# A hybrid RWKV, attention and expert block: gating shared by two engines, and four changes of order

## The chip, the cores and the metric

The kernel runs on one core of a Trainium2 chip. The metric is the device time of one execution in microseconds (us). Before the change it was 2046.03 us, the median of three runs (2045.47 to 2049.38). The engines are TensorE (PE; PEld is its weight load), VectorE (DVE), ScalarE (ACT), GpSimd (POOL) and SyncE (SP), which issues most DMA transfers.

## The reference

The input is 256 tokens of width 2048. One layer is computed: a combined input projection, causal attention with 8 heads of 128, an RWKV-7 time mix with 16 heads of 64, an output projection, and then PEER, a retrieval over 16384 experts of one neuron each, which fills most of the time:

```python
q = (xt @ wq).reshape(T, H, 2, PEER_HALF)
s = jnp.einsum('thpc,hpnc->thpn', q, sub_keys)
sv, si = lax.top_k(s, K)                      # K = 16, of 128 keys, twice
cand = (sv[:, :, 0, :, None] + sv[:, :, 1, None, :]).reshape(T, H, K * K)
best, bi = lax.top_k(cand, K)
expert = (i1 * PEER_NKEYS + i2)
gates = jax.nn.softmax(best, axis=-1)
hpre = jnp.einsum('cd,chkd->chk', xc, u[ec])
act = jax.nn.gelu(hpre, approximate=False) * gc
y = jnp.einsum('chk,chkd->cd', act, v[ec])
```

So for each token 8 heads choose 16 experts each; an expert's gelu is multiplied by its gate, and its row of `v` is added with that weight. A final norm ends it.

## The kernel before, in words

Products in float32 are made of three products of split operands: ScalarE copies a weight into the high part `whi` (L204), VectorE subtracts to get the low part `wlo` (L205), and TensorE multiplies. `prefetch()` does this for a half of 512 KB at a time; three pairs of split buffers stand ready in the stage of the experts, and the list `halves` fixes the order in which weights come from memory through SyncE.

**Stage 1, 0 to about 540 us.** The input projection. `products()` computes three column blocks for each RWKV pair of heads `j` and three for each attention head `h`; each finished one starts a generator (`rwkv`, `attn`) that is put into the list `live`. After every few matmuls of the projection `step_all()` advances up to four generators by a step. First come all eight RWKV blocks, then the eight attention heads. SyncE also writes zeros into `rows_d`, a table in memory (`clear`).

**Stage 2, 540 to 735 us.** Output projection, queries, scores and the first choices.

**Stage 3, 736 to about 1568 us.** `hidden()` multiplies all 16384 expert rows of `u`, 128 keys `i2` of 128 experts each. A key takes 32 pairs of a 512-column (L240) and a 256-column matmul (L242), in two halves of weights. Then ScalarE and VectorE add the two banks into `part` (L1137, L1138), and in the next key ScalarE's gelu (L1122) writes it into the buffer `A` of eight keys. Those buffers, the rows `at` to be scattered and the gates `gt` share one pool of 16 slots.

Beside it three generators run by credit. With each yield of `hidden()` every one gains STEP times its rate, and pays by the number that it yields:

- `both_choices` finds each token's experts (VectorE for the most part).
- `tables` builds for each half of the tokens (a tile `t`) a table of gates over all 128 x 128 experts: VectorE compares (`marks`, L937 and L939), ScalarE weights, TensorE multiplies, GpSimd sums (L951 to L959). Then `places` sorts the experts that are in use: those of the first tile alone, of the second alone, and of both.
- `scatter` handles a key at a time, once its gelu is done. `gated` multiplies the gelus by the gates (L1093), and an indirect DMA issued by GpSimd (L1107) writes the rows to their places in `rows_d`. For every seventh key a new tile `at` is taken and GpSimd copies the seven expert numbers into it (L1085); the seven rows stand side by side in the tile, 256 values and a number each. For every eighth key it loads gates (`gt`, L1075). The last two keys are gated by VectorE and stay in SBUF.

The framework's scheduler sets the final order of each engine's queue from the program and the dependencies, and puts the waits in. An engine runs its queue in order.

**Stage 4, to the end.** Sums over the experts, in 2 blocks from SBUF and 108 blocks of 128 experts (28 for the first tile, 28 for the second, 52 for both). A block's rows are read by SyncE (L1200), its `v` rows are gathered by an indirect DMA of GpSimd (L1205), split (L248, L249) and multiplied (L1192 to L1194) into eight banks. The order ends with blocks for the second tile alone. Then comes a run-time loop over further blocks (L1264), whose count is read from memory and which runs no trip here. The end (L1277 to L1297) adds the banks to the residual, takes the norm and writes the output.

Of the kernel before, what the change touches and what calls it, by code (L numbers as in the profile page):

```python
# [13 lines left out]
I32 = mybir.dt.int32  # L14
# [7 lines left out]
P = 128  # L22
# [132 lines left out]
def block_kernel(ctx: ExitStack, tc: tile.TileContext, x, cols, consts, w_lora, w_gate, w_rkv, w_qkv,  # L155
# [22 lines left out]
    halves = []  # L178
    for i in range(2):
        halves += [(w_lora[m, i].rearrange("p k c -> p (k c)"), HK * LOR) for m in range(2)]  # L180
    for w, n in ((w_gate, 2), (w_rkv, 3 * RJ), (w_qkv, 3 * AH)):
        halves += [(w[m, i].rearrange("p k c -> p (k c)"), HK * P) for m in range(n) for i in range(2)]
    KP = (4, 5, 6, 7, 0, 1, 2, 3)
    halves += [(w_out[m, i].rearrange("p k c -> p (k c)"), 1024) for m in range(4) for i in KP]
    if stage >= 3:
# [447 lines left out]
    def clear(n):  # L633
        for _ in range(n):
            i = len(zero)
            if i < BT // P // 8:
                zero.append(nc.sync.dma_start(gv[:, 8 * i:8 * i + 8, :], zt.unsqueeze(1).to_broadcast([P, 8, ROW])))

    def products():
        pss = [bank(b, [P, S]) for b in ("pw", "px")]  # L640
        for n, _ in enumerate(together([ps[:LOR] for ps in pss], LOR, xhk, xlk)):
            if n == 4:
                nc.sync.dma_start(kb, consts[:, 0:384])
            yield
        nc.sync.dma_start(kr, consts[:, 384:])
        nc.vector.tensor_scalar(bo64, bones, 1.0 / 64, None, op0=ALU.mult)
        psg = [bank("ch", [P, S]) for _ in range(2)]
        yield from gemm(psg[0], P, xhk, xlk)
        for n, _ in enumerate(gemm(psg[1], P, xhk, xlk)):
            if n == 1:  # L650
                first_norm()
                for i in range(2):
                    mixed(pss[i], LOR, cc(C_MW, i), lor[:LOR, i, :])
                mixed(psg[0], P, cc(C_MG, 0), lor[:, 2, :])
            yield
        mixed(psg[1], P, cc(C_MG, 1), lor[:, 3, :])
        state["pools"] = [spl, spl, spare[0]]
        for j in range(RJ):
            while len(live) > 4:
                step_all()  # L660
            got = []
            for i, mu in enumerate((C_MR, C_MK, C_MV)):
                ps = bank("gm")
                yield from gemm(ps, P, xhk, xlk)
                dst = tmp("rkv"[i], "rkv"[i])[:, :S]
                mixed(ps, P, cc(mu, j), dst)
                if j == 0 and i == 0:
                    nc.scalar.activation(lor[:, 2:4, :], lor[:, 2:4, :], AF.Sigmoid)
                    nc.scalar.activation(lor[:LOR, 0, :], lor[:LOR, 0, :], AF.Tanh)
                got.append(dst)  # L670
            live.append(rwkv(j, *got))
            clear(2)
        state["pools"] = [spl]
        for h in range(AH):
            while len(live) > 4:
                step_all()
            got = []
            for i in range(3):
                ps = bank("gm")
                yield from gemm(ps, P, xhk, xlk)  # L680
                dst = tmp("qkv"[i] + "a", "rkv"[i])[:, :S]
                nc.vector.tensor_tensor(dst, ps, rstd1, op=ALU.mult)
                got.append(dst)
            live.append(attn(h, got))
            clear(1)

    def step_all(most=4):
        for g in list(live[:most]):
            if next(g, 0) == 0:
                live.remove(g)  # L690
# [232 lines left out]
    def table(t):  # L923


        while t not in chosen:
            yield 0
        tr = chosen[t]
        b3 = [P, NB, P]
# [75 lines left out]
    def places():  # L1005
# [39 lines left out]
        for t, n, base in ((0, C0, 0), (1, C1, B1)):  # L1045
            V.scalar_tensor_tensor(rank[t], sums[t], off[:, t:t + 1], alone[t], op0=ALU.add, op1=ALU.subtract)
            V.scalar_tensor_tensor(inside[t], rank[t], float(n * P), alone[t], op0=ALU.is_lt, op1=ALU.mult)
            V.tensor_tensor(mid, mid, inside[t], op=ALU.subtract)
            V.scalar_tensor_tensor(tmp_, rank[t], float(base), inside[t], op0=ALU.add, op1=ALU.mult)
            V.tensor_tensor(pos, pos, tmp_, op=ALU.add)  # L1050
            yield 1.5
        V.tensor_tensor_scan(sums[2], ones, mid, 0.0, op0=ALU.mult, op1=ALU.add)
        V.tensor_copy(tot[:, 2:3], sums[2][:, P - 1:P])
        ps = ranks((2, 1))
# [25 lines left out]
    def gated(i2, eng=nc.gpsimd):  # L1080

        if i2 % 7 == 0:
            rows[0] = big("at")
            n = min(7, NKEY - i2)
            eng.tensor_copy(rows[0][:, 0:n * ROW].rearrange("p (n c) -> p n c", c=ROW)[:, :, T].bitcast(I32),  # L1085
                                  eint[:, i2:i2 + n])
        g = gates_of(i2 // 8)
        if i2 % 8 == 1:
            gates_of(i2 // 8 + 1)
            gts.pop(i2 // 8 - 1, None)  # L1090
        at = rows[0][:, i2 % 7 * ROW:(i2 % 7 + 1) * ROW]
        k = i2 % 8
        eng.tensor_tensor(at[:, 0:T].rearrange("p (q t) -> p q t", q=KT),  # L1093
                          As[i2 // 8][:, k, :].rearrange("p (q t) -> p q t", q=KT),
                          g.rearrange("p q (t b) -> p q t b", b=8)[:, :, :, k], op=ALU.mult)
        return at

    def scatter():
        while "places" not in chosen:
            yield 0  # L1100
        gates_of(0)
        yield 0
        for i2 in range(NKEY - DN):
            while hid["n"] <= i2:
                yield 0
            at = gated(i2)
            s_ = nc.gpsimd.indirect_dma_start(  # L1107
                out=rows_d, out_offset=bass.IndirectOffsetOnAxis(ap=place[:, i2:i2 + 1], axis=0),
                in_=at, in_offset=None)
            for z_ in done:  # L1110
                tc.declare_no_dep(s_.ins, z_.ins, reason="other rows")
            for z_ in zero:
                tc.add_manual_dep(s_.ins, z_.ins.name, SYNC, reason="zeros first")
            done.append(s_)
            yield 1.5


    summed = []
# [24 lines left out]
    def both_choices():  # L1143
        yield from finding
        for t in (1, 0):
            yield from choose(t)

    def tables():
        for t in (1, 0):
            yield from table(t)  # L1150
        yield from places()

    STEP = 1.44
    beside = [[both_choices(), 0.55, 0.0], [tables(), 0.38, 0.0], [scatter(), 1.0, 0.0]]

    def run(b, most=None):
        while b[2] > 0 and (most is None or most > 0):
# [85 lines left out]
    for k in range(len(order) + 5):  # L1243
# [13 lines left out]
        if k >= 5:  # L1257
            j = k - 5
            for t in order[j][1]:
                block((t,), *cut[j], ends[t] == j)  # L1260

    count = nc.values_load(nblk[0:1, 0:1], min_val=0, max_val=128,
                           skip_runtime_bounds_check_because="a count of at most 16384 experts in blocks of 128")
    with tc.For_i(MID, count, 1) as i:  # L1264
        ag, _ = rows_at(i * P + BM)
        block((0, 1), *divided(ag, gather(ag)), True)

    gf = mp.tile([P, D], F32, tag="ml", name="gf")
    nc.gpsimd.dma_start(gf, final_g.rearrange("(o d) -> o d", o=1).to_broadcast([P, D]))
# [53 lines left out]
```

## Time and profile before

| what | value |
|---|---|
| median of three runs | 2046.03 us |
| profiled execution | 2048.21 us |
| its span in the profile | 2046.3 us |
| TensorE busy | 1935.7 us (95%) |
| VectorE busy | 1437.7 us (70%) |
| ScalarE busy | 1062.9 us (52%) |
| GpSimd busy | 712.1 us (35%) |
| DMA | 443.91 MB, 217 GB/s over the span |

The span is what the profile's rows cover; the execution's own time is 1.9 us longer, for what lies around it. Busy shares are means over stages that differ, so they only say where to look: TensorE first. A stage is then read by itself, by the busy time of each engine in it, by what TensorE waited for, and by the instructions around a wait. `out<-in` names the tiles that an instruction writes and reads; idle time stands with the engine and line that ended it.

### The profile page before, as it was taken

To read this page: it belongs to the slowest core of one execution; us is meant where nothing else is said; L and a number is where in the kernel's file an instruction comes from. 1 tells how busy PE (TensorE), PEld (TensorE's weight loads), DVE (VectorE), ACT (ScalarE), POOL (GpSimd) and SP (SyncE) were. 2 spreads that over 40 slices of the span, in tenths; PEclk is the share of its full clock that TensorE was granted. 3 is DMA by queue.
4 is the path that set the end of the run, shared out by engine and by line. 5 is a ranking of instruction groups with operands and counts; after the bars stand their busy time and mean duration, and the time that the engine had idled before them with its cause. 6 is when DMAs were issued, how large, how long until landed. Compare 5 with 4: busy or idle time off the path is not lost. (4 is left out here: it accounts for less than half of the span.)

```text
span 2046.3 us, 31447 instructions
## 1 busy us (share of the span) xinstructions
PE 1935.7 (95%) x11804; PEld 1723.3 (84%) x11804; DVE 1437.7 (70%) x2090; ACT 1062.9 (52%) x1696; POOL 712.1 (35%) x654
## 2 busy tenths in 40 slices
PE   7888999999999999999999999887998999999996
PEld 6788999999879998878888888776887788888885
DVE  6766878766556888999878866544755666666665
ACT  4534554345455444677676744433444555555554
POOL 7211211100000000023424269998986333333322
PEclk9999999999999999999999999998999999999998
DMA  8999322225576666556666678786888887878783
GB/s 248 258 247 246 98 87 87 88 83 146 190 227 198 184 180 188 173 175 197 215 195 217 196 237 264 248 267 229 270 267 271 343 284 280 296 286 293 281 297 141
DMA packets 135291, 443.91 MB, mean 217 GB/s; under 512 B 14369, under 2 KB 52257, under 8 KB 118497
## 3 DMA queue, kind: packets, MB, share of 16 engines
q1 hardware_dynamic: 106992, 289.24, 47.7%
q0 software_dynamic: 28144, 152.65, 20.4%
q8 instruction: 93, 1.52, 0.3%
q14 instruction: 62, 0.50, 0.1%
HBM read 380.07 MB, written 61.76 MB: 216 GB/s over the span
## 5 line engine op out<-in xcount | busy, mean ns | idle before, releaser
L205 DVE TENSOR_TENSOR wlo<-raw,whi 128x1024 fp32r<-128x1024 f32 (+1 forms) x408 | 569.6, 1402 | 301.1 <-ACT whi L204 291.9
L240 PE MATMUL ps_gm<-nx,whi 128*128 128x512 f32 x2048 | 731.8, 400 | 24.9 <-ACT whi L204 21.9
L204 ACT ACTIVATE whi<-raw 128x1024 fp32r<-128x1024 f32 (+1 forms) x408 | 429.5, 1055 | 384.2 <-issue 89.5
L242 PE MATMUL ps_gm<-nx,wlo 128*128 128x256 f32 x2048 | 579.4, 283 | 14.2 <-DVE wlo L205 14.2
L240 PEld LDWEIGHTS ps_gm<-nx,whi 128*128 128x128 f32 x2048 | 387.8, 189 | 112.6 <-ACT whi L204 22.6
L242 PEld LDWEIGHTS ps_gm<-nx,wlo 128*128 128x128 f32 x2048 | 390.3, 191 | 20.1 <-DVE wlo L205 19.7
L249 DVE TENSOR_TENSOR vlo<-vraw,vhi 128x2048 fp32r<-128x2048 f32 x108 | 247.9, 2297 | 151.6 <-ACT vhi L248 146.1
L248 ACT ACTIVATE vhi<-vraw 128x2048 fp32r<-128x2048 f32 x108 | 205.9, 1913 | 156.3 <-DVE vlo L249 146.8
L1205 POOL DMA_INDIRECT vraw<-in_v_dram,ag x108 | 145.1, 1343 | 294.8 <-PE ps_gm L1194 210.0
L218 PE MATMUL ps_gm<-xh,whi 128*128 128x256 f32 x640 | 192.7, 301 | 0.8 <-ACT whi L204 0.8
L220 PE MATMUL ps_gm<-xh,wlo 128*128 128x256 f32 x640 | 185.1, 289 | 3.2 <-DVE wlo L205 3.1
L219 PE MATMUL ps_gm<-xl,whi 128*128 128x256 f32 x640 | 185.6, 290 | 0.0
L1107 POOL DMA_INDIRECT rows_d<-at,place x126 | 169.5, 1345 | 36.9 <-POOL at L1093 15.8
L951 POOL TENSOR_TENSOR mt<-gc 128x1024 f32<-128x1024 f32 x16 | 39.7, 2482 | 345.5 <-ACT gc L979 345.5
L1122 ACT ACTIVATE A<-part 128x256 f32<-128x256 f32 x128 | 53.1, 415 | 166.7 <-DVE part L1138 131.3
L1093 POOL TENSOR_TENSOR at<-A,gt 128x256 f32<-128x256 f32 x126 | 129.2, 1041 | 5.4 <-DMA gt<-gate_d 3.6
L220 PEld LDWEIGHTS ps_gm<-xh,wlo 128*128 128x128 f32 x640 | 122.8, 192 | 4.6 <-DVE wlo L205 4.2
L218 PEld LDWEIGHTS ps_gm<-xh,whi 128*128 128x128 f32 x640 | 122.9, 192 | 1.9 <-ACT whi L204 1.2
L219 PEld LDWEIGHTS ps_gm<-xl,whi 128*128 128x128 f32 x640 | 122.9, 192 | 0.7
L807 POOL DMA_DIRECT2D skb<-in_sk_dram x16 | 8.6, 540 | 250.7 <-ACT mh L248 167.7
L945 ACT ACTIVATE ob<-ob,pick 128x128 f32<-128x128 f32 x256 | 83.9, 390 | 19.6 <-DVE ob L937 19.6
L373 POOL TENSOR_TENSOR df<-ext 128x256 f32<-128x256 f32 (+1 forms) x28 | 23.8, 850 | 155.3 <-DVE ext L371 142.4
(1521 smaller groups left out, 3925.5 us busy)
## 6 DMA issues: line engine op xcount, KB each, us to landing
raw<-in_u_dram SPq DMA_DIRECT2D x256, 512.0 KB, 4.1
raw<-in_w_rkv_dram SPq DMA_DIRECT2D x48, 512.0 KB, 7.3
raw<-in_w_qkv_dram SPq DMA_DIRECT2D x48, 512.0 KB, 3.6
rows_d<-zt SPq DMA_DIRECT2D x23, 1028.0 KB, 15.8
raw<-in_w_out_dram SPq DMA_DIRECT2D x32, 512.0 KB, 3.9
raw<-in_wq_dram SPq DMA_DIRECT2D x32, 512.0 KB, 3.6
gate_d<-gc SPq DMA_DIRECT2D x16, 1024.0 KB, 6.5
gt<-gate_d POOLq DMA_DIRECT2D x16, 1024.0 KB, 9.0
```

The lines of the kernel that those rows point to most:

```text
L204: nc.scalar.activation(hi[:, :n], raw[:, :n], AF.Copy)
L205: state["dve"] = nc.vector.tensor_tensor(lo[:, :n], raw[:, :n], hi[:, :n].bitcast(F32), op=ALU.subtract)
L218: nc.tensor.matmul(ps, a, xh(kt), start=first and k == 0, stop=False)
L219: nc.tensor.matmul(ps, a, xl(kt), start=False, stop=False)
L220: state["mm"] = nc.tensor.matmul(ps, b, xh(kt), start=False, stop=last and k == HK - 1)
L240: nc.tensor.matmul(ps.rearrange("p z t -> p (z t)"), hi[:, k * P:(k + 1) * P], x_.rearrange("p z t -> p (z t)"), start=i + k == 0, stop=Fa ...
L242: state["mm"] = nc.tensor.matmul(ps[:, 0, :], lo[:, k * P:(k + 1) * P], x_[:, 0, :], start=False, stop=i == 1 and k == HK - 1, skip_group_ ...
L248: nc.scalar.activation(hi, src, AF.Copy)
L249: nc.vector.tensor_tensor(lo, src, hi.bitcast(F32), op=ALU.subtract)
L1093: eng.tensor_tensor(at[:, 0:T].rearrange("p (q t) -> p q t", q=KT), As[i2 // 8][:, k, :].rearrange("p (q t) -> p q t", q=KT), g.rearrange( ...
L1107: s_ = nc.gpsimd.indirect_dma_start(out=rows_d, out_offset=bass.IndirectOffsetOnAxis(ap=place[:, i2:i2 + 1], axis=0), in_=at, in_offset=None)
L1205: nc.gpsimd.indirect_dma_start(out=raw, out_offset=None, in_=vf, in_offset=bass.IndirectOffsetOnAxis(ap=ag[:, T:ROW].bitcast(I32), axis=0))
```

## The change

Five edits. (1) The input projection takes RWKV and attention blocks in turn from the third on, with the weights in the same order. (2) A table is begun only when the choices of both tiles are made; the rates of choices and tables rise from 0.55 and 0.38 to 0.6 and 0.45. (3) A step of `places` and a scattered key pay 2.6 and 2.3 in place of 1.5. (4) Keys with an even number are gated by VectorE, the odd ones by GpSimd as before; the copy of the expert numbers stays with GpSimd. (5) The run-time loop stands after the 36th of the 108 blocks, and its matmuls don't end the accumulation any more. Line numbers rise by 4, from the middle of `products` on by 8, and by 11 behind the loop (L1093 is now L1101, L1107 is L1115, L1295 is L1306).

```diff
-    for w, n in ((w_gate, 2), (w_rkv, 3 * RJ), (w_qkv, 3 * AH)):
-        halves += [(w[m, i].rearrange("p k c -> p (k c)"), HK * P) for m in range(n) for i in range(2)]
+    ORDER = [("r", 0), ("r", 1)] + [x for j in range(2, RJ) for x in (("r", j), ("a", j - 2))] + [("a", AH - 2), ("a", AH - 1)]
+    blocks_ = [(w_gate, m) for m in range(2)]
+    for what, n in ORDER:
+        blocks_ += [((w_rkv if what == "r" else w_qkv), 3 * n + i) for i in range(3)]
+    halves += [(w[m, i].rearrange("p k c -> p (k c)"), HK * P) for w, m in blocks_ for i in range(2)]
...
+        for k, (what, n) in enumerate(ORDER):
+            while len(live) > 4:
+                step_all()
+            if what == "a":
+                state["pools"] = [spl]
+            yield from (pair if what == "r" else head)(n)
...
     def table(t):
-        while t not in chosen:
+        while 0 not in chosen or 1 not in chosen:
             yield 0
...
-            yield 1.5
+            yield 2.6
...
         if i2 % 7 == 0:
             rows[0] = big("at")
             n = min(7, NKEY - i2)
-            eng.tensor_copy(rows[0][:, 0:n * ROW].rearrange("p (n c) -> p n c", c=ROW)[:, :, T].bitcast(I32),
+            nc.gpsimd.tensor_copy(rows[0][:, 0:n * ROW].rearrange("p (n c) -> p n c", c=ROW)[:, :, T].bitcast(I32),
                                   eint[:, i2:i2 + n])
...
-            at = gated(i2)
+            at = gated(i2, nc.gpsimd if i2 % 2 else nc.vector)
...
-            yield 1.5
+            yield 2.3
...
-    beside = [[both_choices(), 0.55, 0.0], [tables(), 0.38, 0.0], [scatter(), 1.0, 0.0]]
+    beside = [[both_choices(), 0.6, 0.0], [tables(), 0.45, 0.0], [scatter(), 1.0, 0.0]]
...
-    count = nc.values_load(nblk[0:1, 0:1], min_val=0, max_val=128,
-                           skip_runtime_bounds_check_because="a count of at most 16384 experts in blocks of 128")
-    with tc.For_i(MID, count, 1) as i:
-        ag, _ = rows_at(i * P + BM)
-        block((0, 1), *divided(ag, gather(ag)), True)
+        if k == 40:
+            count = nc.values_load(nblk[0:1, 0:1], min_val=0, max_val=128,
+                                   skip_runtime_bounds_check_because="a count of at most 16384 experts in blocks of 128")
+            with tc.For_i(MID, count, 1) as i:
+                rows[2] = rows[1]
+                ag, _ = rows_at(i * P + BM)
+                rows[1] = rows[2]
+                block((0, 1), *divided(ag, gather(ag)), False)
```

How the queues stand now is shown at three places. The first is VectorE's queue of the changed kernel while keys 89 to 91 are multiplied; the gatings (L1101) in it are those of rows 42, 44 and 46, 48 to 54, 56, and 58 and 60 (the number behind `A_` and `gt_` names the buffer of eight keys):

```order
L1101 TENSOR_TENSOR at<-A_10687,gt_13855 128x256
L209 TENSOR_TENSOR wlo<-raw,whi 128x1024
L1101 TENSOR_TENSOR at<-A_10687,gt_13855 128x256 x2
L209 TENSOR_TENSOR wlo<-raw,whi 128x1024
L1146 TENSOR_TENSOR part<-part,ps_gm 128x256
L1101 TENSOR_TENSOR at<-A_11261,gt_14042 128x256 x4
L209 TENSOR_TENSOR wlo<-raw,whi 128x1024
L1101 TENSOR_TENSOR at<-A_11845,gt_14219 128x256
L209 TENSOR_TENSOR wlo<-raw,whi 128x1024
L1146 TENSOR_TENSOR part<-part,ps_gm 128x256
L209 TENSOR_TENSOR wlo<-raw,whi 128x1024
L1101 TENSOR_TENSOR at<-A_11845,gt_14219 128x256 x2
```

In the kernel before, this piece of the queue holds nothing but two splits and one `part` in turn. Ten gatings now stand among five splits, and what follows a gating waits with it.

The second place is GpSimd's queue at the same rows, first before the change:

```order
L1075 DMA gt_13659<-gate_d 128x16x128
L1093 TENSOR_TENSOR at<-A_10788,gt_13541 128x256
L1085 COPY at<-eint 128x7
L1093 TENSOR_TENSOR at<-A_10788,gt_13541 128x256
L1107 DMA rows_d<-at,place 39936x257 x2
L1093 TENSOR_TENSOR at<-A_10788,gt_13541 128x256 x2
L1107 DMA rows_d<-at,place 39936x257 x2
L1093 TENSOR_TENSOR at<-A_10788,gt_13541 128x256 x2
```

and now, first from the scatters of rows 37 to 41 on:

```order
L1115 DMA rows_d<-at,place 39936x257 x5
L1083 DMA gt_14042<-gate_d 128x16x128
L1093 COPY at<-eint 128x7 x2
L1083 DMA gt_14219<-gate_d 128x16x128
L1115 DMA rows_d<-at,place 39936x257
L1101 TENSOR_TENSOR at<-A_10687,gt_13855 128x256
```

and then, after four more scatters and two gatings, to the copy for the tile of rows 56 to 62:

```order
L1115 DMA rows_d<-at,place 39936x257 x2
L1101 TENSOR_TENSOR at<-A_11261,gt_14042 128x256
L1115 DMA rows_d<-at,place 39936x257 x2
L1101 TENSOR_TENSOR at<-A_11261,gt_14042 128x256
L1115 DMA rows_d<-at,place 39936x257 x2
L1101 TENSOR_TENSOR at<-A_11261,gt_14042 128x256
L1115 DMA rows_d<-at,place 39936x257 x2
L1101 TENSOR_TENSOR at<-A_11261,gt_14042 128x256
L1093 COPY at<-eint 128x7
```

A pair of gatings stood to each pair of scatters, now one. The copy of the expert numbers (L1093) of the tile that begins with row 56 stands behind the scatter of row 54, and VectorE's gating of row 58 waits for it.

The third is the end of VectorE's queue, now:

```order
L253 TENSOR_TENSOR vlo<-vraw,vhi 128x2048
L253 TENSOR_TENSOR al__19315<-ag,ah 128x256
L1306 TENSOR_TENSOR yr<-yr,ps_mm 128x512
L1306 TENSOR_TENSOR yr<-yr,ps_pw 128x512
L1306 TENSOR_TENSOR yr<-yr,ps_ch 128x512
L253 TENSOR_TENSOR al__19335<-ag,ah 128x256
L1301 TENSOR_TENSOR z_19383<-yr,gf 128x512
L1306 TENSOR_TENSOR yr<-yr,ps_ch 128x512
```

Before, all additions of banks (there L1295) stand behind the loop, which is the last thing before them:

```order
L249 TENSOR_TENSOR al__19327<-ag,ah 128x256
L249 TENSOR_TENSOR vlo<-vraw,vhi 128x2048
L1264 REGISTER_ALU
L1264 COMPARE_AND_BRANCH
L1264 UNCONDITIONAL_BRANCH
L1295 TENSOR_TENSOR yr<-yr,ps_mm 128x512
L1295 TENSOR_TENSOR yr<-yr,ps_pw 128x512
L1295 TENSOR_TENSOR yr<-yr,ps_ch 128x512
```

Now those of the first tile (banks `ps_mm`, `ps_pw`, `ps_ch`) stand among the splits of the last blocks, and the loop lies two thirds of the blocks ahead of them.

## Rows read from the trace of the kernel before

**Rows 1.** The span by stage: window, length, busy (x instructions) by engine, PEclk, DMA share, GB/s.

```profile
0.00:200.00 200.00, 164.67 (x1251) 157.84 (x1252) 134.59 (x220) 86.95 (x137) 68.42 (x107) 0.97 1.01 252
200.00:540.00 340.00, 335.06 (x2695) 325.22 (x2694) 249.42 (x494) 159.40 (x301) 37.26 (x46) 1.00 0.35 104
855.00:960.00 105.00, 96.79 (x593) 84.99 (x592) 104.38 (x167) 74.28 (x157) 29.21 (x18) 1.00 0.58 181
960.00:1190.00 230.00, 230.00 (x1443) 205.24 (x1442) 186.71 (x190) 165.50 (x356) 83.99 (x56) 1.00 0.66 206
1370.00:1400.00 30.00, 12.50 (x57) 10.25 (x56) 5.40 (x7) 5.27 (x8) 26.71 (x30) 0.66 0.54 174
1400.00:1565.00 165.00, 159.19 (x901) 137.20 (x900) 105.08 (x84) 74.95 (x112) 147.29 (x131) 1.00 0.83 268
```

**Rows 2.** Timeline of TensorE, two successive pairs: start us, us, engine line.

```profile
1366.04 0.40 PE L240 MATMUL ps_gm<-nx,whi 128*128 128x512 f32 x1
1366.38 0.39 PE L240 MATMUL ps_gm<-nx,whi 128*128 128x512 f32 x1
```

**Rows 3.** Line L240 from 1220 to 1565 us: PE, PEld busy, PEclk, DMA, GB/s.

```profile
1220.00:1565.00 345.00, 310.68 (x876) 166.50 (x875) 0.96 0.79 257
```

**Rows 4.** Lines of 1220 to 1560 us: count | busy us, mean ns | idle before.

```profile
L240 PE MATMUL ps_gm<-nx,whi 128*128 128x512 f32 x861 | 305.9, 399 | 24.9 <-ACT whi L204 21.9 <-DVE part L1138 2.9
L242 PE MATMUL ps_gm<-nx,wlo 128*128 128x256 f32 x862 | 244.6, 284 | 6.0 <-DVE wlo L205 6.0
L205 DVE TENSOR_TENSOR wlo<-raw,whi 128x1024 fp32r<-128x1024 f32 x108 | 179.1, 1672 | 144.5 <-ACT whi L204 136.7 <-PE ps_gm L240 6.0 <-PE ps_gm L242 1.4
L1107 POOL DMA_INDIRECT rows_d<-at,place x124 | 166.8, 1345 | 36.3 <-POOL at L1093 15.2 <-issue 14.9 <-DVE place L1060 5.9
L1093 POOL TENSOR_TENSOR at<-A,gt 128x256 f32<-128x256 f32 x118 | 119.5, 1027 | 3.2 <-DMA gt<-gate_d 1.5
L1075 POOL DMA_DIRECT2D gt<-gate_d x14 | 16.9, 1207 | 0.0
```

**Rows 5.** What TensorE waited for, 1340 to 1410 and 1200 to 1340: us, times, longest.

```profile
PE ps_gm L240 <- ACT whi L204: 17.0, 1, 17.0
PE ps_gm L240 <- ACT whi L204: 4.9, 1, 4.9
```

**Rows 6.** Timeline of ScalarE and TensorE around 1390 us; in brackets the idle time before.

```profile
1390.30 0.42 ACT L1122 ACTIVATE A<-part 128x256 f32<-128x256 f32 x1 [21.80 <-POOL at L1093]
1374.40 0.28 PE L242 MATMUL ps_gm<-nx,wlo 128*128 128x256 f32 x1
1391.71 0.80 PE L240 MATMUL ps_gm<-nx,whi 128*128 128x512 f32 x1 [17.03 <-ACT whi L204]
```

**Rows 7.** Lines of GpSimd from 1376 to 1391.2 us, while VectorE and ScalarE wait.

```profile
L1093 POOL TENSOR_TENSOR at<-A,gt 128x256 f32<-128x256 f32 x8 | 6.6, 851 | 0.1
L1107 POOL DMA_INDIRECT rows_d<-at,place x6 | 6.0, 994 | 1.4 <-issue 0.9 <-POOL at L1093 0.5
L1085 POOL COPY at<-eint 128x7 int32<-128x7 int32 x1 | 0.2, 203 | 0.0
```

**Rows 8.** Tile `at`, whole span: duration ns min/median/max, first and last start.

```profile
L1093 POOL TENSOR_TENSOR at<-A,gt x126: 843/942/1997, 1205.2 to 1562.2; 128x256 f32<-128x256 f32 x126
L1107 POOL DMA_INDIRECT rows_d<-at,place x126: 961/1054/2045, 1219.8 to 1563.4; - x126
L1093 DVE TENSOR_TENSOR at<-A,gt x2: 621/662/704, 1567.1 to 1572.9; 128x256 f32<-128x256 f32 x2
```

**Rows 9.** Lines of 735 to 855 us, a stretch in which GpSimd does nothing.

```profile
L205 DVE TENSOR_TENSOR wlo<-raw,whi 128x1024 fp32r<-128x1024 f32 x44 | 53.4, 1215 | 12.1 <-ACT whi L204 12.0
```

**Rows 10.** Timeline of the end: the last matmul and VectorE's additions.

```profile
2028.80 0.39 PE L1194 MATMUL ps_gm<-vhi,al__19260 128*128 128x512 f32 x1
2029.58 0.69 DVE L1295 TENSOR_TENSOR yr<-yr,ps_mm 128x512 f32<-128x512 f32 x1 [7.86 <-PEq L1264]
2037.63 0.67 DVE L1295 TENSOR_TENSOR yr<-yr,ps_gm 128x512 f32<-128x512 f32 x1
```

More of the change, by code (lines that the diff above doesn't have):

```diff
@@ L657, in products, with pair @@
         state["pools"] = [spl, spl, spare[0]]
-        for j in range(RJ):
-            while len(live) > 4:
-                step_all()
+        def pair(j):
             got = []
@@ L672, in products, with head @@
             clear(2)
[L673 to L676, printed above, removed]
+        def head(h):
             got = []
```

## The prediction

> **What bounds the kernel now.** I read the page's busy shares first (TensorE busy 95% of the span), then the busy time of each engine by stage, to find the places where TensorE is not busy. In the table of stages [rows 1] the reader is to see four things. From 0 to 200 us TensorE is busy 164.67 us while the DMA engines are full (share 1.01, 252 GB/s); from 200 to 540 it is busy 335.06 of 340. From 855 to 960, while the choices are made, VectorE is the full one (104.38 of 105) and TensorE has 96.79. From 960 to 1190 TensorE is full and VectorE has 43 us to spare. From 1220 to 1565, the stretch of the scatters, GpSimd is the fullest engine beside TensorE (147.29 of 165 in its last part), and there lies the one large loss.
>
> That loss is worked out from the hidden products alone. One pair of them, a 512-column and a 256-column matmul, is issued every 0.346 us when nothing is in the way [rows 2], so half a key (8 pairs) takes 2.77 us and a key 5.54. The stretch has 876 pairs [rows 3], at 0.346 us 303 of its 345 us: 42 us are lost. The lines of that stretch put 24.9 + 6.0 = 31 us of this down to waits [rows 4]; the other 11 are the clock, which stood at 0.66 of full speed in the 30 us around the longest wait [rows 1]. So an idle microsecond costs about 0.35 us more in clock. The waits of TensorE name ScalarE's `whi` [rows 5], and the stretch by engine shows what is behind it [rows 6]: ScalarE's gelu waited 21.80 us for a GpSimd gating, because the slot it writes, one of 16 that the buffers share, was still being read; the weight splits stood behind it on ScalarE; TensorE stopped for 17.03 us. That its wait is 4.8 us shorter than ScalarE's is its slack: the split weights that lie ready. I take 5.5 us, two halves.
>
> **The change, part by part.** The sum is made against the profiled execution, 2048.2 us, which is 2.2 above the median of the runs.
>
> *Gating on VectorE.* 63 of 126 gatings leave GpSimd. There one takes 1.03 us in this stretch [rows 4], 0.85 while VectorE sleeps [rows 7]; a scatter takes 1.345 us [rows 4] and (6.0 + 1.4)/6 = 1.23 with its gaps while VectorE sleeps [rows 7]. GpSimd is relieved of 63 x 1.03 = 65 us, and by the order its place in the gatings is then ahead of every gelu that had to wait: the old stalls go, worth up to 42 us. VectorE pays 63 x 0.66 [rows 8] = 42 us, which its free time covers (it was busy 105.08 of 165 [rows 1]).
>
> But VectorE takes its instructions in order, and the order puts the gatings there in five bursts (rows 0 to 20, 22 to 40, 42 to 62, 64 to 82, 84 to 104), among the splits that TensorE lives on. From the second row of a tile of seven on, a gating writes where GpSimd's copy of the expert numbers writes too, and that copy stands in GpSimd's queue behind its scatters. Take the third burst. Rows 42 to 56 bring VectorE to row 58, whose copy stands behind 55 scatters and 28 gatings of GpSimd; when row 42 was gated, GpSimd can have had at most 42 and 21 behind it, for its next scatter needs row 42. So 13 scatters, 7 gatings, two loads of gates at 1.2 us [rows 4] and some copies stand between, and behind the waiting gating stand the next split and the next `part` sum, which ScalarE's gelu and TensorE wait for. Only 5 splits come before it, and with the slack they feed TensorE 5 x 2.77 + 5.5 = 19.4 us. Over the five bursts, counted in the same way (to rows 16, 36, 58, 78 and 100), that is 13, 14, 13, 14 and 13 scatters, 7 gatings each, 10 loads and about 2 us of copies in all, against 4, 6, 5, 6 and 6 splits: 67 scatters to 27 splits.
>
> The price of a scatter in such a burst lies between 1.23 (VectorE asleep) and 1.345 + 0.25 of gap = 1.59 (VectorE at work; of the 36.3 us of gaps before 124 scatters 5.9 are the first one's [rows 4]). VectorE would work half of a burst, so I take the middle, 1.41, and 1.0 for a gating; a copy takes 0.2 [rows 7]: 94.5 + 35 + 12 + 2 = 143 us, against 27 x 2.77 + 5 x 5.5 = 102 of feed. TensorE idles 41. To this come the times in which GpSimd waits in turn for a VectorE row that stands behind a split (each up to 1.67 [rows 4], 27 of them): I take a fifth, 9 us. Idle 50, clock 0.35 x 50 = 17, together 67 where 42 were lost: **+25**. Bounds: all of GpSimd at its sleeping price and never waiting gives 82.4 + 29.8 + 14 - 102 = 24 idle, 32 with the clock, so -10; the dear price and a slack of one half in each burst give 106.5 + 36 + 14 - 89 = 67 idle, 91 with the clock, +49.
>
> The trace says why VectorE's work matters to this price: a split takes 1215 ns while GpSimd rests [rows 9] and 1672 beside it [rows 4]. The Trainium skill (SBUF — State Buffer, Who interferes with whom) has it that a VectorE instruction with two SBUF inputs and a GpSimd instruction that reads SBUF lock each other out of a port they share; the trace agrees in direction, 1215 against 1672 ns. By that rule a VectorE that waits leaves GpSimd wholly free, and the sum would take the sleeping price, -10 in place of +25.
>
> *The loop in the middle.* Before, every engine passes the loop after the last block, and only then starts what ends the kernel: TensorE ends at 2029.19, VectorE adds the first bank at 2029.58 and the last at 2037.63, and the span ends 8.7 us later [rows 10]. Moved to behind block 35, the loop no longer holds the first tile's end, which the order now has ahead of the last blocks (these are for the second tile alone). What is left behind the last matmul is 0.4 + 8.7 = 9.1 in place of 17.1: **-8**. The new cost is a meeting of engines at block 35. It took 0.4 us at the end [rows 10]; nothing shows it with gathers and splits in flight, but the splits of two more blocks and gathers up to block 39 stand ahead of it. I take +1, between 0.4 and the 8 us that would eat the gain. Net **-7**.
>
> *Tables behind both choices, and the two rates.* The comparisons that build the tables leave a stretch where VectorE is full and enter one where it has 43 us to spare [rows 1]. At most the 8 us that TensorE lacks between 855 and 960 can be won; the choices are also drawn more densely (0.6 for 0.55), which fills VectorE again. **-2**, from -6 to +8 (the same shortage once more).
>
> *RWKV and attention blocks in turn.* The stretch to 200 us is full of DMA, and the same zero-fills and weights are asked for there; after it TensorE lacks 5 us in 340 [rows 1]. The end of the last chains now lies beside the output projection in part. **0**, from -6 to +6. *The dearer yields* only set the order read above: nothing of their own.
>
> Sum: 2048.2 + 25 - 7 - 2 + 0 = 2064.2; by the median, **2062 us**.
>
> **The rivals.**
> *GpSimd is fast enough (faster).* If VectorE's sleep makes GpSimd as quick as while VectorE slept in the old stall, the gating is worth -10 and the sum is 2029, by the median 2027; with the medians of 1.054 and 0.942 us [rows 8] and hidden gaps it is 70.6 + 33 + 14 - 102 = 16 idle, 21 with the clock, -21, so 2016. It decides below a scatter of 1.22 us, gaps included: then GpSimd's time in the bursts falls under 131 us, TensorE idles 29 + 9 us, and with the clock 51 us, which the old 42 and the other parts' 9 pay. For it: the sleeping price is a row. Against it: VectorE sleeps only while it waits.
> *The trade comes out even.* Burst waits and clock of about 51 us cancel the old stalls together with the -9 of the other parts: 2046, within 0.2%.
> *The first stage gains.* Chains of two kinds in turn fill TensorE better; at most the 5 us after 200 and some of the 35 before it, if those were not the DMA's: 10 us less than the forecast, 2052, and faster than before only where the gating part comes out some 8 us better too.
> *The meeting in the middle is dear.* If all engines drain and the first gathers start afresh, it takes the whole gain of 8: 2069.
>
> **How the numbers follow.** Forecast (bursts wait, +25 with its spread) 0.56, among it the dear meeting; GpSimd fast enough 0.31; even 0.09; first stage 0.04. The likeliest case alone runs from 2046 to 2090. The range reaches down to the fast GpSimd's far end and a few us of the first stage's, 2012, and up to 2085, leaving about 0.1 below and 0.07 above. A measurement of this kernel can tell 0.2%, 4 us. Faster 0.34, same 0.10, slower 0.56.
>
> **What would show it.** Right: VectorE's gatings with idle time ended by GpSimd's copy (some 10 us each, in five places), TensorE waiting behind them for `wlo` or `whi`, and a granted clock under 1 after each; gelu no longer waiting for a GpSimd gating. The span's end 9 us behind the last matmul, and a gap of about 1 us at block 36. Wrong: those waits under 5.5 us, or scatters of 1.0 us throughout, or a new gap of many microseconds at the loop.

## The result and the profile after

The changed kernel takes 2079.82 us (median of 4 runs, 2073.55 to 2083.13), the one before 2045.85 (4 runs). The ratio is 1.0159, 95% interval 1.013 to 1.0187: **slower by 34 us**, where 16 had been forecast. The profiled execution took 2083.13 us, its span is 2081.3, 35.0 more than before.

Where the 35.0 us come from is read from four marks in both timelines: the first and last hidden product, the end of the last matmul, the end of the span. The hidden products begin at 733.2 us (735.9 before), the last one starts at 1610.4 (1567.7), TensorE ends at 2071.96 (2029.19), the span at 2081.3 (2046.3). So the stages ahead of the hidden products took 2.7 us less, the hidden products 45.4 more, the sums 0.1 more, the end 7.8 less.

The stages of the changed kernel, to be set beside [rows 1]; columns as there:

```profile
0.00:200.00 200.00, 170.27 (x1269) 163.74 (x1270) 130.20 (x215) 80.80 (x127) 64.81 (x98) 0.93 1.00 250
855.00:960.00 105.00, 104.45 (x634) 92.29 (x633) 95.38 (x140) 71.07 (x142) 14.60 (x10) 1.00 0.63 187
960.00:1190.00 230.00, 222.44 (x1402) 197.76 (x1400) 191.49 (x192) 162.65 (x367) 95.31 (x62) 1.00 0.64 203
1220.00:1320.00 100.00, 78.28 (x417) 66.99 (x417) 51.82 (x68) 34.73 (x52) 73.43 (x67) 0.92 0.70 221
1345.00:1380.00 35.00, 19.36 (x102) 16.43 (x101) 16.62 (x22) 9.17 (x15) 30.76 (x24) 0.79 0.54 163
1405.00:1445.00 40.00, 27.99 (x136) 23.42 (x135) 19.77 (x25) 13.37 (x20) 32.29 (x29) 0.86 0.57 187
```

TensorE now stops several times between 1220 and 1510 us, and the granted clock is below 1 in each of the last three stretches. Such a figure is a mean of the clock's two levels, 2.4 GHz and 1.2 GHz: the first matmul behind the wait of the third burst, shown below, took 0.79 us, where one takes 0.40 and 0.39 in [rows 2]. Of the line of the hidden products, L244 now, from 1231 to 1611 us:

```profile
1231.00:1611.00 380.00, 314.04 (x852) 167.46 (x851) 0.92 0.71 229
```

852 pairs at 0.346 us are 295 of 380 us: 85 are lost, where it was 42 [rows 3]. (A key takes 16 pairs, 8 for each half of its weights, and not the 32 of the description ahead: the line has 2048 matmuls for 128 keys.) The lines from 1220 to 1610 us, to be set beside [rows 4], say where:

```profile
L244 PE MATMUL ps_gm<-nx,whi 128*128 128x512 f32 x880 | 324.2, 411 | 27.6 <-DVE part L1146 27.6
L246 PE MATMUL ps_gm<-nx,wlo 128*128 128x256 f32 x880 | 255.1, 290 | 33.8 <-DVE wlo L209 33.7
L1115 POOL DMA_INDIRECT rows_d<-at,place x126 | 171.7, 1363 | 130.5 <-DVE at L1101 70.0 <-issue 55.7 <-POOL at L1101 3.4
L1101 POOL TENSOR_TENSOR at<-A,gt 128x256 f32<-128x256 f32 x63 | 58.8, 937 | 16.0 <-ACT A L1130 14.9
L1101 DVE TENSOR_TENSOR at<-A,gt 128x256 f32<-128x256 f32 x64 | 45.7, 749 | 82.3 <-POOL at L1093 76.2 <-DMA gt<-gate_d 3.0 <-ACT A L1130 2.4
```

VectorE's gatings stood still for 76.2 us until GpSimd's copy of the expert numbers (L1093) was done, in ten waits, and TensorE for 27.6 + 33.8 = 61.4 us behind VectorE's `part` and `wlo`. GpSimd in turn waited 70.0 us for rows of VectorE. No gelu waits for GpSimd any more [rows 6]; in the list of waits of the same window ScalarE's gelu stands behind VectorE's `part` instead:

```profile
ACT A L1130 <- DVE part L1146: 154.9, 52, 16.0
DVE at L1101 <- POOL at L1093: 76.2, 10, 16.6
```

No value passes from that copy to the gating that waits for it. The copy writes the number behind the 256 values of each of seven rows, a gating writes the 256 values of one. The ten waits are those of rows 8, 16, 30, 36, 58, 72, 78, 92, 100 and 114, each the first row of VectorE behind the first row of its tile; the rows with which these tiles begin, where they are VectorE's (14, 28, 56, 70, 98, 112), were gated 9 us and more ahead of the same copies. This fits a dependency that goes by the whole stretch from the copy's first element to its last, in which the later rows lie. That the gating writes where the copy does, as the prediction has it, is so of the stretch and not of the elements.

One burst by itself, the third. The timelines of VectorE, GpSimd and TensorE there (start us, us; in brackets the idle time before; GpSimd's rows first from the dear part, then from the cheap one):

```profile
1342.89 0.69 DVE L1101 TENSOR_TENSOR at<-A,gt 128x256 f32<-128x256 f32 x1
1348.99 2.47 DVE L1101 TENSOR_TENSOR at<-A,gt 128x256 f32<-128x256 f32 x4
1356.06 1.23 DVE L209 TENSOR_TENSOR wlo<-raw,whi 128x1024 fp32r<-128x1024 f32 x1 [1.44 <-ACT whi L208]
1373.86 1.15 DVE L1101 TENSOR_TENSOR at<-A,gt 128x256 f32<-128x256 f32 x2 [16.57 <-POOL at L1093]
1374.92 1.22 DVE L209 TENSOR_TENSOR wlo<-raw,whi 128x1024 fp32r<-128x1024 f32 x1
1376.06 0.41 DVE L1146 TENSOR_TENSOR part<-part,ps_gm 128x256 f32<-128x256 f32 x1
```

```profile
1347.31 2.36 POOL L1115 DMA_INDIRECT rows_d<-at,place  x1 [0.81 <-DVE at L1101]
1349.97 5.16 POOL L1115 DMA_INDIRECT rows_d<-at,place  x1 [0.30 <-issue]
...
1363.89 1.00 POOL L1115 DMA_INDIRECT rows_d<-at,place  x1 [0.17 <-issue]
1365.20 0.96 POOL L1115 DMA_INDIRECT rows_d<-at,place  x1 [0.30 <-issue]
1366.19 0.86 POOL L1101 TENSOR_TENSOR at<-A,gt 128x256 f32<-128x256 f32 x1
...
1373.62 0.21 POOL L1093 COPY at<-eint 128x7 int32<-128x7 int32 x1
```

```profile
1360.73 0.28 PE L246 MATMUL ps_gm<-nx,wlo 128*128 128x256 f32 x1
1376.53 0.79 PE L244 MATMUL ps_gm<-nx,whi 128*128 128x512 f32 x1 [15.51 <-DVE part L1146]
```

From the gating of row 42 (1342.89) to the copy that releases row 58 (1373.83) GpSimd took 30.9 us; the working had 143/5 + 9/5 = 30.4. That these are so near is luck: the two loads of gates in the working (2.4 us) had been issued before the burst, since they stand ahead of row 42's scatter and don't need that row, and the 13 scatters took 1.75 us each with the idle time before them, where 1.41 had been taken. Over all five bursts, from the first gating to the copy that ends the last long wait, GpSimd took 146.4 us for 152. While VectorE worked, two scatters took 2.36 and 5.16 us; once it stood still, two scatters and a gating took 3.3 us together, the sleeping price of [rows 7]. TensorE had work until 1361.0, 18.1 us for the 19.4 of the working, and began again not with the copy but 2.7 us later, after the gatings, the split and the `part` that stood behind it.

The end, to be set beside [rows 10]:

```profile
2063.72 0.68 DVE L1306 TENSOR_TENSOR yr<-yr,ps_mm 128x512 f32<-128x512 f32 x1
2071.57 0.39 PE L1202 MATMUL ps_gm<-vhi,al__19335 128*128 128x512 f32 x1
2073.45 0.68 DVE L1306 TENSOR_TENSOR yr<-yr,ps_gm 128x512 f32<-128x512 f32 x1
```

The first tile's additions start 8.2 us ahead of TensorE's last end, and 9.3 us lie behind it instead of 17.1. What the loop costs in the middle is one row of TensorE, the first matmul behind it:

```profile
1788.79 0.50 PE L1200 MATMUL ps_mm<-vhi,ah 128*128 128x512 f32 x1 [1.99 <-issue]
```

### The profile page after: what moved, and what is told of

Same layout as the page of the kernel before. It is cut to its first block, busy times and chain, and to the rows that moved or that the text cites. A ratio compares the mean times of both kernels' runs of the same rounds, so it can differ in the third digit from the quotient of the medians.

```text
span 2081.3 us, 31433 instructions
## 1 busy us (share of the span) xinstructions
PE 1948.1 (94%) x11804; PEld 1734.5 (83%) x11804; DVE 1430.2 (69%) x2152; ACT 1067.4 (51%) x1702; POOL 638.6 (31%) x592
## 5 line engine op out<-in xcount | busy, mean ns | idle before, releaser
L244 PE MATMUL ps_gm<-nx,whi 128*128 128x512 f32 x2048 | 742.2, 405 | 30.7 <-DVE part L1146 30.7
L209 DVE TENSOR_TENSOR wlo<-raw,whi 128x1024 fp32r<-128x1024 f32 (+1 forms) x418 | 527.6, 1266 | 270.0 <-ACT whi L208 264.7
L244 PEld LDWEIGHTS ps_gm<-nx,whi 128*128 128x128 f32 x2048 | 393.5, 192 | 122.8 <-DVE part L1146 34.0
L222 PE MATMUL ps_gm<-xh,whi 128*128 128x256 f32 x720 | 222.4, 309 | 1.9 <-ACT whi L208 1.8
L1115 POOL DMA_INDIRECT rows_d<-at,place x126 | 171.7, 1363 | 130.5 <-DVE at L1101 70.0
L224 PE MATMUL ps_gm<-xh,wlo 128*128 128x256 f32 x720 | 208.0, 289 | 2.6 <-DVE wlo L209 2.0
L223 PE MATMUL ps_gm<-xl,whi 128*128 128x256 f32 x720 | 208.5, 290 | 0.0
L222 PEld LDWEIGHTS ps_gm<-xh,whi 128*128 128x128 f32 x720 | 139.8, 194 | 3.8 <-ACT whi L208 2.9
L224 PEld LDWEIGHTS ps_gm<-xh,wlo 128*128 128x128 f32 x720 | 139.5, 194 | 3.7 <-DVE wlo L209 2.6
L223 PEld LDWEIGHTS ps_gm<-xl,whi 128*128 128x128 f32 x720 | 140.0, 194 | 0.8
L1101 DVE TENSOR_TENSOR at<-A,gt 128x256 f32<-128x256 f32 x65 | 46.3, 747 | 82.8 <-POOL at L1093 76.2
L945 DVE TENSOR_TENSOR ob<-iota,pick 128x512 f32<-128x512 f32 x64 | 71.6, 1119 | 3.2 <-POOL act L965 3.2
```

What stands on the lines that cost most here:

```text
L209: state["dve"] = nc.vector.tensor_tensor(lo[:, :n], raw[:, :n], hi[:, :n].bitcast(F32), op=ALU.subtract)
L222: nc.tensor.matmul(ps, a, xh(kt), start=first and k == 0, stop=False)
L223: nc.tensor.matmul(ps, a, xl(kt), start=False, stop=False)
L224: state["mm"] = nc.tensor.matmul(ps, b, xh(kt), start=False, stop=last and k == HK - 1)
L244: nc.tensor.matmul(ps.rearrange("p z t -> p (z t)"), hi[:, k * P:(k + 1) * P], x_.rearrange("p z t -> p (z t)"), start=i + k == 0, stop=Fa ...
L1115: s_ = nc.gpsimd.indirect_dma_start(out=rows_d, out_offset=bass.IndirectOffsetOnAxis(ap=place[:, i2:i2 + 1], axis=0), in_=at, in_offset=None)
```

## The experiments on the gating

The runs were made in three groups on two chips, and the kernel before took medians of 2040.43, 2057.71 and 2042.1 us beside them, so each run is given as a ratio to the runs of before in its own group. For the changed kernel that is 1.0159. Line numbers move with each edit; the names of the tiles tell what a line is.

**All gatings back on GpSimd**, the rest of the change kept:

```diff
-            at = gated(i2, nc.gpsimd if i2 % 2 else nc.vector)
+            at = gated(i2)
-            nc.gpsimd.tensor_copy(rows[0][:, 0:n * ROW]
+            eng.tensor_copy(rows[0][:, 0:n * ROW]
```

> The changed kernel with all gatings back on GpSimd. Queue theory (VectorE waits in order behind GpSimd's copies): the 76 us of VectorE's waits for the copy and the 61 us of TensorE's waits go, with their clock. GpSimd then has 126 scatters and 126 gatings, at 1.345 + 0.25 + 1.03 us some 331 us from the first scatter at 1231, so it ends near 1561 and the sums start near 1580: about 2036 us, 2026 to 2046, and TensorE may wait at the start of the sums instead of in the middle. Rival (the other parts together cost the time): it stays above 2065.

Measured: 2046.66 us, 1.0039 (1.0021 to 1.0056). So undoing the split takes 0.012 of 0.0159 away, some 24 us, and the other four parts together, with all gatings on GpSimd, are 0.4% slower than the kernel before, not faster by 9 us as in the sum. TensorE's waits from 1220 us on:

```profile
PE ps_mm L1200 <- ACT ah L252: 15.7, 1, 15.7
PE ps_ch L1200 <- ACT whi L208: 12.0, 1, 12.0
PE ps_gm L246 <- DVE wlo L209: 9.2, 12, 2.7
PE ps_mm L1200 <- ACT vhi L252: 5.2, 1, 5.2
```

The stalls among the hidden products are gone, and the waits of 15.7, 12.0 and 5.2 us at the first sums (L1200) have taken their place: GpSimd scattered until 1578.0 us, 31 us behind the last hidden product. That was expected; that the kernel is slower was not. GpSimd's first scatter came 496.4 us after the first hidden product (729.4 to 1225.8), where it was 483.9 before (735.9 to 1219.8). The two parts run by themselves below take this up.

**The split alone**, on the kernel before (the two lines of the gating in the diff of the change):

> The kernel before with the split of the gating alone. Queue theory: the same waits for GpSimd's copy as in the changed kernel, without the 8 us at the end and the 3 us of the first stages: 2080 to 2095 us. Rival (the dearer yields make the bursts): no bursts, VectorE waits under 25 us in all, 2010 to 2040.

Measured: 2082.91 us, 1.0211 (1.0179 to 1.0243), within the expectation. VectorE's waits from 1220 to 1620 us and TensorE's from 1220 to 1700:

```profile
DVE at L1093 <- POOL at L1085: 71.8, 10, 12.0
DVE at L1093 <- DMA gt<-gate_d: 9.9, 4, 4.1
```

```profile
PE ps_gm L242 <- DVE wlo L205: 32.6, 9, 6.4
PE ps_gm L240 <- DVE part L1138: 28.5, 5, 8.8
```

The waits are those of the changed kernel, with the old yields too; the yields do not make them. 0.0211 is 43 us, the same as the lines of the hidden products give for the split in the changed kernel (85 lost for 42). And beside the split the other four parts take time off: 1.0159 with them, 1.0211 without, some 11 us, which is near the 9 of the sum, though the two intervals overlap a little.

**VectorE's rows in tiles of their own.** Even and odd keys get a tile `at` each, into which the engine that gates also copies the numbers:

```diff
-        if i2 % 7 == 0:
-            rows[0] = big("at")
-            n = min(7, NKEY - i2)
-            nc.gpsimd.tensor_copy(rows[0][:, 0:n * ROW]
+            key, left = i2 % 2, i2 // 2 % 7
+            src = eint.rearrange("p (a b) -> p a b", b=2)[:, i2 // 2:(NKEY - DN) // 2, i2 % 2]
+        if left == 0:
+            rows[0, key] = big("at")
+            n = min(7, src.shape[1])
+            eng.tensor_copy(rows[0, key][:, 0:n * ROW]
```

> The changed kernel, with VectorE's rows in tiles of their own into which VectorE copies the expert numbers, so no gating of VectorE waits for a copy of GpSimd; the loads of the gates still stand in GpSimd's queue between scatters. Queue theory: waits for the copy 0, waits for the gates' loads in their place, shorter by a few scatters in each burst: TensorE idle 25 to 45 instead of 61, 2040 to 2065 us. Rival (two engines reading SBUF hinder each other, and that is the cost): nothing changes, 2074 to 2084.

Measured: 2065.66 us, 1.0128 (1.0091 to 1.0164): by the intervals not to be told from the changed kernel, and TensorE still waited 35.4 + 21.9 = 57 us, more than the 25 to 45 expected. By the time alone the rival stands. VectorE's first waits, 1220 to 1620 us:

```profile
DVE wlo L209 <- ACT whi L208: 97.9, 76, 4.0
DVE at L1106 <- DMA gt<-gate_d: 69.2, 8, 15.7
```

The copy is gone from the list, and the loads of the gates, which GpSimd issues in order between its scatters, hold VectorE for 69.2 us in its place. That one wait takes the place of the other speaks for the queue; by itself it doesn't yet exclude that the engines hinder each other.

**And the gates loaded by SyncE.** The same kernel with one word changed:

```diff
-            nc.gpsimd.dma_start(gts[g], gate_d[:, :, g * P:(g + 1) * P])
+            nc.sync.dma_start(gts[g], gate_d[:, :, g * P:(g + 1) * P])
```

> As the run with tiles of VectorE's own, and the loads of the gates issued by SyncE instead of GpSimd, so VectorE's gatings wait for nothing in GpSimd's queue but freed slots. Queue theory: TensorE's waits from 1230 on under 15 us, GpSimd ends its scatters near 1510 to 1530, 1995 to 2015 us. Rival (the engines hinder each other): scatters of several us and TensorE waits stay, over 2050. A third way: SyncE's queue of weights waits behind a load whose slot is not free; then ScalarE waits for raw, 2020 to 2050.

Measured: 2022.89 us, 0.9926 (0.9904 to 0.9948), faster than the kernel before, though not by as much as expected. GpSimd scattered until 1541 us and not to 1510 or 1530. The time lies where the third way put it, and ScalarE waited 60.3 us for `raw` from 1220 to 1620; but only 2.3 us of TensorE's waits are put down to `whi`, so the trace doesn't show that this is what was missing. TensorE's waits from 1220 to 1700 us, and GpSimd's two lines from 1220 to 1620:

```profile
PE ps_gm L246 <- DVE wlo L209: 8.3, 8, 1.9
PE ps_gm L244 <- DVE part L1151: 4.2, 3, 3.7
PE ps_mm L1205 <- ACT ah L252: 3.6, 1, 3.6
PE ps_gm L244 <- ACT whi L208: 2.3, 1, 2.3
```

```profile
L1120 POOL DMA_INDIRECT rows_d<-at,place x126 | 182.6, 1449 | 48.1 <-issue 20.0 <-DVE at L1106 18.1 <-POOL at L1106 7.2
L1106 POOL TENSOR_TENSOR at<-A,gt 128x256 f32<-128x256 f32 x63 | 60.8, 980 | 42.3 <-DMA gt<-gate_d 23.8 <-ACT A L1135 17.7
```

This shows the cause. The same engine gates the same rows, and the scatters are even dearer (1449 ns, 1363 in the changed kernel), so that the engines hinder each other isn't by itself what cost the time; but VectorE no longer waits in its queue for something far back in GpSimd's, and TensorE's waits fall from 61 us to some 15 among the hidden products, and the ratio from 1.0159 to 0.9926. One thing isn't separated: the same word takes 16 loads off GpSimd, some 20 us at 1.22 us each, and the loads on SyncE without the split were not run. The step from 1.0128 to 0.9926 is 41 us, so that relief could be at most half of it.

## The experiments on the other parts

**The loop alone:**

> The kernel before with the run-time loop behind block 35 and nothing else. By the prediction's term: 8 us less behind the last matmul and 1 to 2 us of meeting at block 36: 0.35% faster, 7 us, from 5 to 8. Rival (the meeting is dear): no gain or slower, with a gap of 8 us and more of TensorE at block 36.

Measured: 2053.35 us, 0.998 (0.9964 to 0.9996), 4 us. The gap at block 36 is the same as in the changed kernel, 1.99 us. The interval reaches from 1 to 7 us and so holds both the expected 7 and less. In its profiled execution 13.0 us lie behind the last matmul (2038.76 to 2051.8), where the changed kernel has 9.3: there the rest is missing. The output's writes are issued until 6.6 us behind the last matmul, 6.3 in the changed kernel, so it lies behind them; what the span's end waits for there stays open.

**The tables and the rates alone** (0.6 and 0.45, both choices awaited):

> The kernel before with tables behind both choices and the rates 0.6 and 0.45 alone. By the prediction's term: 2 us less. Rival, from the trace of the changed kernel: the time won for TensorE between 855 and 960 us is lost again between 960 and 1190, the first scatter comes 8 to 13 us later in the stage, and since GpSimd's chain of scatters ends last before the sums, the kernel is 5 to 13 us slower.

Measured: 2061.61 us, 1.0022 (1.001 to 1.0033), slower by 4.5 us: the rival's direction, a little below its range. Two stages of its trace, to be read as [rows 1]:

```profile
855.00:960.00 105.00, 104.50 (x625) 91.88 (x624) 97.41 (x160) 66.69 (x128) 12.65 (x8) 1.00 0.64 192
960.00:1190.00 230.00, 223.27 (x1407) 198.67 (x1406) 192.43 (x197) 165.70 (x375) 91.73 (x61) 1.00 0.64 199
```

The 8 us that TensorE lacked in the first stretch were won, and 7 were lost in the second, where it had lacked none. There it waited for VectorE's `part` and `wlo` and for ScalarE, which empties the banks of the tables' products (960 to 1190 us):

```profile
PE ps_gm L240 <- DVE part L1138: 2.8, 4, 1.2
PE ps_pw L969 <- ACT gc L979: 2.3, 1, 2.3
PE ps_gm L242 <- DVE wlo L205: 1.3, 2, 0.7
```

The first scatter comes 489.7 us after the first hidden product, 5.8 later than before.

**The dearer yields alone:**

> The kernel before with the dearer yields of places and scatter alone. By the prediction: no cost of its own. The order asks for 39 scatters before the gelu of key 96 where before it asked for 63, so the stalls of 17 and 5 us go; GpSimd's chain is as long as before, so the time comes back as a wait at the start of the sums: within 4 us of before. Rival (the stalls were a loss of their own): 25 to 42 us faster. If places ends later, as much slower as the first scatter is later in the stage.

Measured: 2062.65 us, 1.0018 (1.0003 to 1.0034), 4 us slower. TensorE's waits from 1220 us on:

```profile
PE ps_ch L1192 <- ACT whi L204: 13.9, 1, 13.9
PE ps_mm L1192 <- ACT ah L248: 13.5, 1, 13.5
PE ps_mm L1192 <- ACT vhi L248: 7.4, 1, 7.4
```

The 17 and 4.9 us of the old stalls [rows 5] are gone and stand at the sums instead, since GpSimd scattered until 1584.4 us, 31 us past the last hidden product. So those stalls weren't a loss of their own in the kernel before: GpSimd's chain of 126 scatters and 126 gatings (343.6 us from 1219.8 to 1563.4 there, 348.7 here) filled the stretch, and where TensorE waits for it is a matter of order. The first scatter is 9.0 us later in the stage than before, and a chain that ends last makes the kernel later with it.

**The blocks in turn alone:**

> The kernel before with RWKV and attention blocks in turn and nothing else. By the prediction's term: 0, from -6 to +6. From the traces of the runs that hold it: the hidden products start 2 to 3 us earlier, which is 0.1% and can't be told from no change by the times; the trace shows it by the start of the output projection, some 6 us earlier. Rival (chains in turn fill TensorE): 5 us and more.

Measured: 2038.16 us, 0.9984 (0.9973 to 0.9996), 3 us faster, in the expected size. The four parts beside the gating thus measure -0.20, -0.16, +0.22 and +0.18% one by one, near nothing in sum, and +0.39% together without the split.

**A mended version.** The kernel before with the split, tiles of VectorE's own, gates loaded by SyncE, the loop and the blocks in turn; tables, rates and yields as before:

> Rows of VectorE in tiles of its own, gates loaded by SyncE, gatings split, loop behind block 35, blocks in turn; tables, rates and yields as before the change. If the first scatter is again some 12 us earlier than with the changed tables and yields, and GpSimd's chain ends before the hidden products: 1995 to 2012 us on a chip with 2040 before. Rival: the smaller yields let the slots wait for more scatters, the old stalls come back in part: 2015 to 2030.

Measured: 2029.11 us, 0.9858 (0.983 to 0.9886), **1.4% faster than the kernel before**: 29 us, where 28 to 45 were expected. TensorE waited 9.6 + 5.7 us among the hidden products, its largest waits there, and no gelu stall of many microseconds came back. It beats both kernels. It differs from the run with own tiles and the gates on SyncE in tables, rates and yields alone, and 0.9858 is below that run's 0.9926 with intervals that don't meet; where the difference falls stays open.

**The gates two groups ahead.** The same with `gates_of(i2 // 8 + 2)`:

> The mended kernel with the gates loaded two groups of keys ahead. Its VectorE waited 21 us for gates and its GpSimd 9; if that still holds TensorE, those waits go and the time falls by 5 to 15 us against the mended kernel (1.42% under before), to some 1.7 to 2.1% under before. Rival (the gates' slot is missing elsewhere: the gelu of key 96 now stands behind 68 scatters where 63 did): stalls of gelu come back, and it is no faster than the mended one.

Measured: 2021.32 us, 0.9904 (0.9883 to 0.9924): not the gain that was expected, and by the ratios, whose intervals just touch, some 0.5% slower than the mended version. No gelu waits for GpSimd, so the rival's reason isn't what the trace shows either. The profiled execution, the slowest of the six (2033.61 us), has a new wait of TensorE,

```profile
PE ps_gm L243 <- ACT whi L207: 12.7, 3, 11.8
```

and ScalarE there waited up to 14.9 us for a weight from memory. That a load of the gates held up the weights in SyncE's queue while its slot was in use would fit this, but no run shows it.

## Why the prediction was right in kind and wrong in size

- **The cause was right.** VectorE's gatings wait in five bursts behind GpSimd's copies, `part` and splits stand behind them, the clock falls, the gelu's stalls are gone. Undoing the split takes some 24 of the 34 us away, and mending the queue takes all of it.
- **The step that failed is the size of that term, the gating on VectorE.** +25 was forecast; it was +43 (85 us lost for 42). Of the 18 us that are missing, 5 are idle time in the bursts, 6 are other waits and 7 are the clock. In the bursts TensorE's nine waits of over 2 us are 55 us for 50. The working let TensorE go on with the copy that frees VectorE; it goes on only after the gating and the split or `part` behind the copy, 1.8 to 4.3 us later (2.7 in the third burst), and behind the last waits of the five bursts this is 15 us that had been put at nothing. That only 5 of them show is luck: GpSimd took 146 us for 152, and TensorE worked 106 us where 102 were counted. In four of the five bursts VectorE waits twice and not once. The other waits, 6 us, had been let go with the old stalls, and stayed. And what is left for the clock is 85 - 61 = 24 us for 17: there was more idle time, and 0.39 for an idle microsecond and not 0.35.
- **The upper bound held** (+49), and the range held the time; the likeliest value was too near its middle. That the whole is off by no more than this one term is luck too: the other terms came to -8 for -9, but not one by one, as follows.
- **The weighing of the port rule.** While VectorE stood still, GpSimd ran at its sleeping price, as the Trainium skill (SBUF — State Buffer, Who interferes with whom) would have it; while it worked, single scatters took up to 5.16 us, beyond the 1.59 that the working allowed. Over the five bursts a scatter took 1.57 us with the idle time before it, so the dear end of the two prices and not their middle; GpSimd's time came out near all the same because fewer other instructions stood in the bursts (5 loads of gates for 10).
- **The loop**: -7.8 behind the last matmul for -8, +2.0 in the middle for +1: right. **The first stages**: -2.7 for 0, in the range.
- **Tables, rates and yields**: -2 and "nothing of their own" were wrong by themselves. In the changed kernel the hidden products ahead of the scatters took some 2 us more (45.4 in all, 43 of it the split's). By itself each is about 0.2% slower, for the tables with TensorE's gain of 8 us given back in the next stretch, for both with a later first scatter, in kernels in which GpSimd's chain ends last. What they do to the time of the changed kernel, where the bursts set it, no run shows by itself.
- **"The old stalls go, worth up to 42 us"** was wrong for the yields, though the stalls went: as long as GpSimd does all gatings, the wait only moves to the sums. What the relief of GpSimd can be worth shows in the mended version, 29 us with the loop and the blocks in turn among them.

## What to carry to other kernels

Moving work to an engine with free time can cost more than it gives, as here, when what it waits for is queued behind other work of the engine that was relieved: look in the order for every instruction of the new owner that needs one of the old owner's, and at what stands behind it. Ask also whether a value passes between the two at all, or whether they only share a tile. Give the moved work its own tiles and its own loads first. And before counting a stall as a gain to be had, ask whether the chain behind it would end any earlier; if not, the stall turns up at the next stage.

## What had not been expected of the hardware

A scatter issued by GpSimd, 0.96 us when VectorE rests, took 5.16 us while VectorE ran gatings and splits with little pause from 1348.99 us on; it ended at 1355.13. In the whole trace of the changed kernel the 45 scatters beside which VectorE ran no TENSOR_TENSOR instruction took 0.99 us in the mean and 1.04 at most, the 81 others 1.57. In the run with the gates on SyncE the mean rose to 1449 ns, with 119 of the 126 beside VectorE, and the kernel was faster all the same. The meeting of all engines at a run-time loop without trips cost TensorE 2.0 us in the middle of the sums, in each of three profiles read for it (the changed kernel, the loop alone, the mended version).
